# Mixers' queries, keys and probabilities turned in 32x32 squares through HBM, low weight parts last in each unit, and blank matmuls at the opening

## The chip, the cores and the metric

One core of one Trainium2 chip. The metric is the device time of one execution in microseconds, the median of three runs. The core has TensorE (PE), VectorE (DVE), ScalarE (ACT), GpSimd (POOL) and SyncE (SP), which run side by side and wait for one another by semaphores; transfers run on 16 DMA engines and are issued from a queue of SP or POOL here.

## The reference, cut to what matters

Two layers on 256 tokens of width 2048, float32. Layer 0 mixes by retention (8 heads) and neighbourhood attention (8 heads), layer 1 by differential attention (8 heads with two softmax maps each). Each layer then attends to 256 memory tokens and runs a SwiGLU FFN.

```
for i in range(DEPTH):
    h = rms_norm(x, norm_mix_g[i])
    x = x + (retention_na_mixer if i % 2 == 0 else diff_attention_mixer)(h, ...)
    m = rms_norm(mem, norm_mem_g[i])
    x = x + memory_cross_attention(rms_norm(x, norm_xattn_g[i]), m, ...)
    x = x + swiglu_ffn(rms_norm(x, norm_ffn_g[i]), w_ffn_in[i], w_ffn_out[i])
# differential attention, per head:
a = softmax(q0 k0^T * scale + alibi) - lam * softmax(q1 k1^T * scale + alibi)
o = rms_norm(a @ v, out_g) * (1 - lam_init)
```

Queries and keys are normalised per head of 128 in both attentions.

## The kernel before, in words

**Products.** Every projection is a `gemm` (L297) over units. A unit is 256 rows of a weight by 512 columns, against all 256 tokens. Weight and activation are each held as a high part (rounded to fp32r) and a low part (the rest), and three products are summed: high by high (L321), high by low weight (L322), low by high weight (L323). With two halves of tokens (t) and two k-tiles (j) a unit is twelve matmuls with 512 columns each. There are 864 units. `prepare` (L269) loads raw weights by SP's queue, 512 rows at a time, ScalarE casts the high part `wh` (L292), and VectorE subtracts to get the low part `wl` (L293); `LOOK` = 2 units are prepared ahead.

**Side work.** Norms, attention heads and gates are generators in a list (`Side`, L33). After each unit `pump` runs one step of the first task that is due and ready; a `yield n` puts the next step n units later. At most `CAP` = 5 tasks may be under way. `drain` runs named tasks to their end at once. The order of the instructions on each engine is the order in which this writes them.

**Turning.** A matmul needs its operands with features on the partitions, so queries, keys, probabilities, heads' outputs and gates are turned. Two ways are in the kernel. In the first PE transposes 128x128 blocks against an identity into PSUM: `turn` (L345) for queries, keys (`z`) and gates (`sg`), four to a group; `transpose_p` (L545) for probabilities (`pr`); L702 for the outputs of differential attention (`do`). ScalarE and VectorE then take the high and low parts out of PSUM. In the second, `regroup` (L377), used for blocks of x and the FFN's activations, VectorE transposes 32x32 squares within partitions (L389), SP's queue writes the block to a scratch `zd` in HBM (L391), and `LAND` = 2 units later four reads by POOL's queue (L394) bring the squares back to `zz` with partitions exchanged. `MOVE` = 5 units after the write ScalarE and VectorE split it into high and low parts.

**Mixers.** `retention_na` (L613) goes through four groups of four heads, two of neighbourhood attention and two of retention; `normed_T` (L481) squares, sums, takes the reciprocal root by POOL (L334) and scales, `plain_T` does so without a norm, `heads_T` turns. `attend` (L548) makes scores, softmax, turned probabilities and the product. `diff_attention` (L706) goes through four groups b of two heads, by `diff_head` (L662). Their outputs go to `oT`, which the output projection reads. POOL and SP run their queues in order: a DMA that waits for another's landing holds back what stands behind it.

## Time and profile before

| | us |
|---|---|
| median of 3 runs | 2476.86 (2475.91 to 2476.88) |
| profiled execution, its own time | 2475.84 |
| span of the profiled execution | 2474.1 |
| TensorE busy | 2456.3 |
| VectorE busy | 1475.7 |
| ScalarE busy | 1187.0 |
| GpSimd busy | 138.2 |

How to read it: the span runs from the first to the last instruction of one profiled execution. Busy time counts an engine's instructions with overlaps taken once; matmuls are pipelined, so one that is listed with 389 ns can be followed by the next after 227 ns. DMA issues count on POOL as busy; those of SP are only listed as issues. The rows that the prediction rests on stand in a section below.

### The profile page before, as it was taken

How to read it: one execution, taken by the hardware profiler on the slowest of the kernel's cores; microseconds unless marked ns; L12 is line 12 of the kernel's file. 1: busy time of each engine (PE TensorE's matmuls, PEld its weight loads, DVE VectorE, ACT ScalarE, POOL GpSimd, SP SyncE). 2: the span in 40 equal slices, each digit the busy share in tenths (PEclk: the TensorE clock that was granted, in tenths of full speed). 3: DMA queues.
4: the chain of work that ended last, by engine and by line, in shares of the span. 5: the costliest groups of instructions: out<-in, count | busy, mean ns of one | idle time of the engine just before them, and what ended most of it. 6: DMA issues, size and time to landing. Idle time of an engine off the chain costs nothing.

```text
span 2474.1 us, 28641 instructions
## 1 busy us (share of the span) xinstructions
PE 2456.3 (99%) x11184; PEld 2037.1 (82%) x11184; DVE 1475.7 (60%) x1833; ACT 1187.0 (48%) x1538; POOL 138.2 (6%) x215
## 2 busy tenths in 40 slices
PE   8999999999999999999999999999999999999999
PEld 6888888888888888888888888888888888888887
DVE  6775565675655555555567766767655545555554
ACT  6554464564443444444455555655544444443443
POOL 1000001010000000000010000010100000000000
PEclk9999999999999999999999999999999999999999
DMA  8555567656765666566674555675766656665665
GB/s 288 177 169 179 175 226 245 214 192 213 233 216 200 205 212 225 194 198 226 225 241 164 170 170 168 212 249 171 237 222 210 215 188 214 228 206 200 207 217 175
DMA packets 250184, 511.82 MB, mean 207 GB/s; under 512 B 11328, under 2 KB 11968, under 8 KB 250048
## 3 DMA queue, kind: packets, MB, share of 16 engines
q1 hardware_dynamic: 239568, 484.47, 58.5%
q0 software_dynamic: 8320, 23.08, 4.1%
q10 hardware_dynamic: 2160, 2.44, 0.3%
q8 instruction: 87, 1.43, 0.2%
q14 instruction: 49, 0.40, 0.0%
HBM read 486.88 MB, written 23.07 MB: 206 GB/s over the span
## 4 chain that ended last, share of the span: by engine, by line
PE 92%; DMA 3%; DVE 3%; ACT 1%; POOL 1%; issue 0%; ACTq 0%; SPq 0%; POOLq 0%; DVEq 0%
PE acc L322 30%; PE acc L321 30%; PE acc L323 30%; DMA zz<-zd 2%; DVE wl L293 1%; DMA zd<-zz 1%; PE pt L345 1%; ACT wh L292 0%; PE pt L545 0%; PE pa_s L437 0%; PE pa_s L436 0%; DVE x_sb L741 0%; PE pa_s L435 0%; POOL zz L394 0%; PE pa_r L595 0%
## 5 line engine op out<-in xcount | busy, mean ns | idle before, releaser
L293 DVE TENSOR_TENSOR wl<-raw,wh 128x1024 fp32r<-128x1024 f32 (+1 forms) x865 | 1053.7, 1221 | 870.8 <-ACT wh L292 870.4
L292 ACT CAST wh<-raw 128x1024 fp32r<-128x1024 f32 (+1 forms) x865 | 909.1, 1051 | 1158.2 <-PE acc L323 1132.8
L322 PE MATMUL acc<-wl,hTfh 128*128 128x512 f32 x1408 | 547.9, 389 | 0.6 <-DVE wl L293 0.6
L323 PE MATMUL acc<-wh,hTfl 128*128 128x512 f32 x1408 | 547.7, 389 | 0.0
L321 PE MATMUL acc<-wh,hTfh 128*128 128x512 f32 x1408 | 547.7, 389 | 0.0
L321 PE MATMUL acc<-wh,hTh 128*128 128x512 f32 x832 | 332.0, 399 | 9.8 <-ACT wh L292 8.3
L322 PE MATMUL acc<-wl,hTh 128*128 128x512 f32 x832 | 325.7, 391 | 0.9 <-DVE wl L293 0.9
L323 PE MATMUL acc<-wh,hTl 128*128 128x512 f32 x832 | 325.8, 392 | 0.0
L322 PEld LDWEIGHTS acc<-wl,hTfh 128*128 128x128 f32 x1408 | 264.3, 188 | 56.2 <-DVE wl L293 1.4
L323 PEld LDWEIGHTS acc<-wh,hTfl 128*128 128x128 f32 x1408 | 264.3, 188 | 54.9
L321 PEld LDWEIGHTS acc<-wh,hTfh 128*128 128x128 f32 x1408 | 264.3, 188 | 54.9
L322 PE MATMUL acc<-wl,aTh 128*128 128x512 f32 x704 | 274.0, 389 | 0.2 <-DVE wl L293 0.2
L323 PE MATMUL acc<-wh,aTl 128*128 128x512 f32 x704 | 273.9, 389 | 0.0
L321 PE MATMUL acc<-wh,aTh 128*128 128x512 f32 x704 | 273.9, 389 | 0.0
L321 PEld LDWEIGHTS acc<-wh,hTh 128*128 128x128 f32 x832 | 157.2, 189 | 40.0 <-ACT wh L292 8.3
L323 PEld LDWEIGHTS acc<-wh,hTl 128*128 128x128 f32 x832 | 156.7, 188 | 34.0
L322 PEld LDWEIGHTS acc<-wl,hTh 128*128 128x128 f32 x832 | 157.2, 189 | 31.2 <-DVE wl L293 1.8
L394 POOL DMA_DIRECT2D zz<-zd x160 | 87.3, 552 | 1589.9 <-DMA zd<-zz 1410.9
L322 PEld LDWEIGHTS acc<-wl,aTh 128*128 128x128 f32 x704 | 132.1, 188 | 28.2 <-DVE wl L293 0.8
L321 PEld LDWEIGHTS acc<-wh,aTh 128*128 128x128 f32 x704 | 132.1, 188 | 27.5
L323 PEld LDWEIGHTS acc<-wh,aTl 128*128 128x128 f32 x704 | 132.1, 188 | 27.3
L321 PE MATMUL acc<-wh,oTh 128*128 128x512 f32 x256 | 100.2, 392 | 0.0
(189 smaller groups left out, 1940.3 us busy)
## 6 DMA issues: line engine op xcount, KB each, us to landing
raw<-in_w_ffn_in SPq DMA_DIRECT2D x176, 1024.0 KB, 5.1
raw<-in_w_ffn_out SPq DMA_DIRECT2D x88, 1024.0 KB, 5.1
raw<-in_w_in_ab SPq DMA_DIRECT2D x55, 1024.0 KB, 5.2
raw<-in_w_in_c SPq DMA_DIRECT2D x48, 1024.0 KB, 5.2
zd<-zz SPq DMA_DIRECT2D x40, 512.0 KB, 3.8
zz<-zd POOLq DMA_DIRECT2D x160, 128.0 KB, 5.4
raw<-in_w_out_ab SPq DMA_DIRECT2D x16, 1024.0 KB, 5.1
raw<-in_w_xkv SPq DMA_DIRECT2D x16, 1024.0 KB, 5.0
```

The source lines that it names most:

```text
L292: nc.scalar.copy(wh[:, js], raw[:, rs])
L293: nc.vector.tensor_sub(wl[:, js], raw[:, rs], wh[:, js])
L321: nc.tensor.matmul(acc[t], lhsT=hi[:, kt, ts], rhs=wh[:, j], start=first and j == 0, stop=False)
L322: nc.tensor.matmul(acc[t], lhsT=hi[:, kt, ts], rhs=wl[:, j], start=False, stop=False)
L323: nc.tensor.matmul(acc[t], lhsT=lo[:, kt, ts], rhs=wh[:, j], start=False, stop=last and j == 1)
L345: nc.tensor.transpose(pt[:, j, t * P:(t + 1) * P], srcs[t][:, c:c + P], ident)
L394: nc.gpsimd.dma_start(zT[32 * j:32 * j + 32].rearrange("a (i n) -> a i n", i=4), zd[:, :, j].rearrange("i a n -> a i n"))
```

## The change

1. `regroup` takes a number of blocks (`nk` = 4 for 128x1024, 2 for 128x512), a room and a wait. Thirty-five new blocks go through it with `SLOW` = 8 units between write and split: queries and keys of layer 0's four groups and of groups 0 to 2 of differential attention, one of the two gates, the probabilities of 8 neighbourhood heads, and the probabilities and outputs of 6 differential heads. Fifteen are 128x1024 (512 KB), twenty 128x512 (256 KB). The rooms are blocks of `oT` not yet written, `m8` or `qT`.
2. All writes to `zd` (40 before, 75 now) are issued from POOL's queue and not from SP's.
3. In a unit, the eight matmuls with `wh` come first, the four with `wl` last.
4. The operands of a gemm (`pair`) are four tiles of four k-tiles and not one of sixteen.
5. Sixteen 128x128 matmuls of a zeroed tile stand at the opening, ahead of the first unit.
6. `CAP` is 7. In `diff_head` two scalings (32 instructions) go from VectorE to ScalarE; the gains of moved blocks are applied by ScalarE in place.

The diff, cut to its core:

```diff
-LAND, MOVE = 2, 5
+LAND, MOVE, SLOW = 2, 5, 8
-    CAP = 5
+    CAP = 7
...
+    blank = const.tile([P, P], F32, name="blank")
+    nc.vector.memset(blank, 0.0)
+    for _ in range(4):
+        idle = ps_t.tile([P, 2, T], F32, tag="pt", name="idle")
+        for j in range(2):
+            for t in range(2):
+                nc.tensor.matmul(idle[:, j, t * P:(t + 1) * P], lhsT=blank, rhs=blank, start=True, stop=True)
...
-            for t in range(2):
-                ts = slice(t * P, (t + 1) * P)
-                for j in range(2):
-                    kt = kts[u // 2] + 2 * (u % 2) + j
-                    nc.tensor.matmul(acc[t], lhsT=hi[:, kt, ts], rhs=wh[:, j], start=first and j == 0, stop=False)
-                    nc.tensor.matmul(acc[t], lhsT=hi[:, kt, ts], rhs=wl[:, j], start=False, stop=False)
-                    nc.tensor.matmul(acc[t], lhsT=lo[:, kt, ts], rhs=wh[:, j], start=False, stop=last and j == 1)
+            for low in (False, True):
+                for t in range(2):
+                    ts = slice(t * P, (t + 1) * P)
+                    for j in range(2):
+                        hi, lo = src.at(kts[u // 2] + 2 * (u % 2) + j)
+                        if low:
+                            nc.tensor.matmul(acc[t], lhsT=hi[:, ts], rhs=wl[:, j], start=False, stop=last and j == 1)
+                            continue
+                        nc.tensor.matmul(acc[t], lhsT=hi[:, ts], rhs=wh[:, j], start=first and j == 0, stop=False)
+                        nc.tensor.matmul(acc[t], lhsT=lo[:, ts], rhs=wh[:, j], start=False, stop=False)
...
+    def regroup(srcs, room="v", nk=4, wait=MOVE):
+        zt, zT = room_for(room, nk * T)
+        zv = zt.rearrange("p (j k t b) -> p j k t b", j=4, k=nk, t=2)
+        for t in range(2):
+            nc.vector.transpose(zv[:, :, :, t], srcs[t].rearrange("p (k j a) -> p j k a", j=4, a=32))
+        zd = dram.tile([4, 32, 4, nk * 64], F32, tag=f"zd{nk}", name="zd")
+        nc.gpsimd.dma_start(zd.rearrange("i a j n -> (i a) (j n)"), zt)
         yield LAND
         for j in range(4):
             nc.gpsimd.dma_start(zT[32 * j:32 * j + 32].rearrange("a (i n) -> a i n", i=4),
                                 zd[:, :, j].rearrange("i a n -> a i n"))
-        yield MOVE - LAND
+        yield wait - LAND
...
+    def heads_T(zs, dst, g, room=None):
+        if room:
+            zT = yield from regroup(zs, room, wait=SLOW)
+            if g is not None:
+                flat = zT.rearrange("p i k t b -> p (i k t b)")
+                nc.scalar.activation(flat, flat, AF.Copy, scale=g)
+            split_moved(dst, zT)
+            return
...
-        yield 3
-        aT = transpose_p(p0)
+        if room:
+            zT = yield from regroup([p0[:, t] for t in range(2)], "m8", 2, SLOW)
+            aT = tuple(pp.tile([P, 2, T], F32R, name="p" + x) for x in "hl")
+            split_moved(aT, zT)
+        else:
+            yield 3
+            aT = transpose_p(p0)
...
-            nc.vector.tensor_scalar(do[:, t], po[:, t], rr[:, t:t + 1], None, op0=ALU.mult)
+            nc.scalar.activation(do[:, t], po[:, t], AF.Copy, scale=rr[:, t:t + 1])
+        if room:
+            zT = yield from regroup([do[:, t] for t in range(2)], room, 2, SLOW)
...
+            split_moved(oT.at(2 * h, 2), zT)
+            return
```

Where it moves instructions. TensorE, before, in layer 0's first projection: part of one unit, the turning of a block `z` of four heads, and the start of the next unit (`acc_553` and `acc_554` are the two token halves of one accumulator).

```order
L321 MATMUL acc_554<-wh,hTh 128x512
L322 MATMUL acc_554<-wl,hTh 128x512
L323 MATMUL acc_554<-wh,hTl 128x512
L345 MATMUL pt<-ident,z 128x128 x4
L321 MATMUL acc_553<-wh,hTh 128x512
L322 MATMUL acc_553<-wl,hTh 128x512
L323 MATMUL acc_553<-wh,hTl 128x512
```

The same engine after the change, at the same part of the program: one whole unit and the first two rows of the next.

```order
L348 MATMUL acc_585<-wh,hTh 128x512
L349 MATMUL acc_585<-wh,hTl 128x512
L348 MATMUL acc_585<-wh,hTh 128x512
L349 MATMUL acc_585<-wh,hTl 128x512
L348 MATMUL acc_586<-wh,hTh 128x512
L349 MATMUL acc_586<-wh,hTl 128x512
L348 MATMUL acc_586<-wh,hTh 128x512
L349 MATMUL acc_586<-wh,hTl 128x512
L346 MATMUL acc_585<-wl,hTh 128x512 x2
L346 MATMUL acc_586<-wl,hTh 128x512 x2
L348 MATMUL acc_585<-wh,hTh 128x512
```

The low weight part is used from the ninth matmul on and not from the second, and no transposes of `z` stand between units; in the whole program 104 transposes by PE are left of 304.

GpSimd (POOL), before, in differential attention: the end of the reads of x's blocks, and then only the reciprocal roots of the norms of queries and keys (`rr`) and of outputs (`rrd`).

```order
L394 DMA zz<-zd 32x4x256 x4
L334 TENSOR_TENSOR rr<-rr,mhalf 128x8 x2
L334 TENSOR_TENSOR rrd<-rrd,mhalf 128x2 x2
L334 TENSOR_TENSOR rr<-rr,mhalf 128x8 x2
L334 TENSOR_TENSOR rrd<-rrd,mhalf 128x2 x2
```

The same queue after the change, within the same phase (L422 writes a block, L425 reads a part of it back, L360 is the root).

```order
L422 DMA zd<-zz 128x512
L425 DMA zz<-zd 32x4x128 x4
L360 TENSOR_TENSOR rr<-rr,mhalf 128x8
L422 DMA zd<-zz 128x1024
L425 DMA zz<-zd 32x4x256
L422 DMA zd<-zz 128x512
L425 DMA zz<-zd 32x4x256 x2
L425 DMA zz<-zd 32x4x128 x4
L425 DMA zz<-zd 32x4x256
L360 TENSOR_TENSOR rrd<-rrd,mhalf 128x2
L422 DMA zd<-zz 128x512
L425 DMA zz<-zd 32x4x128 x2
```

The roots now stand behind writes and behind reads that wait for a write's landing, and issues of several blocks are interleaved.

## Rows read from the trace of the kernel before

**Rows 1.** Page, part 1: busy time, share of the span, instructions

```profile
PE 2456.3 (99%) x11184; PEld 2037.1 (82%) x11184; DVE 1475.7 (60%) x1833; ACT 1187.0 (48%) x1538; POOL 138.2 (6%) x215
```

**Rows 2.** Windows: busy us of each engine, granted clock, DMA share, GB/s

```profile
124.00:186.00 62.00, 62.00 (x305) 51.86 (x305) 48.37 (x73) 35.29 (x57) 1.63 (x1) 1.00 0.51 168
496.00:558.00 62.00, 61.98 (x309) 51.73 (x309) 48.74 (x78) 38.52 (x72) 7.36 (x13) 1.00 0.61 197
```

**Rows 3.** Waits of TensorE: who for whom, us, times, longest

```profile
PE acc L322 <- DVE wl L293: 2.2, 6, 0.5
...
PE acc L321 <- DVE z L475: 1.5, 2, 0.8
```

**Rows 4.** Groups by form, TensorE: busy us, mean ns, idle before

```profile
L345 PE MATMUL pt<-ident,z 128*128 128x128 f32 x160 | 23.6, 272 | 0.0
```

**Rows 5.** Timeline of TensorE, 115 to 124 us: start, duration, instruction

```profile
115.41 0.39 PE L321 MATMUL acc<-wh,hTh 128*128 128x512 f32 x1
...
118.13 0.39 PE L321 MATMUL acc<-wh,hTh 128*128 128x512 f32 x1
...
119.49 0.60 PE L345 MATMUL pt<-ident,z 128*128 128x128 f32 x4
119.85 0.48 PE L321 MATMUL acc<-wh,hTh 128*128 128x512 f32 x1
...
122.70 0.60 PE L345 MATMUL pt<-ident,z 128*128 128x128 f32 x4
```

**Rows 6.** Timeline of TensorE at the opening, and at the ninth unit

```profile
8.28 0.80 PE L321 MATMUL acc<-wh,hTh 128*128 128x512 f32 x1 [8.28 <-ACT wh L292]
9.49 0.80 PE L322 MATMUL acc<-wl,hTh 128*128 128x512 f32 x1 [0.42 <-DVE wl L293]
10.08 0.63 PE L323 MATMUL acc<-wh,hTl 128*128 128x512 f32 x1
10.51 0.63 PE L321 MATMUL acc<-wh,hTh 128*128 128x512 f32 x1
...
14.32 0.39 PE L321 MATMUL acc<-wh,hTh 128*128 128x512 f32 x1
...
33.36 0.40 PE L321 MATMUL acc<-wh,hTh 128*128 128x512 f32 x1
```

**Rows 7.** Timeline of ScalarE at the ninth unit's weights

```profile
31.01 1.05 ACT L292 CAST wh<-raw 128x1024 fp32r<-128x1024 f32 x1 [3.35 <-DMA raw<-in_w_in_ab]
```

**Rows 8.** Groups by form, VectorE

```profile
L293 DVE TENSOR_TENSOR wl<-raw,wh 128x1024 fp32r<-128x1024 f32 x863 | 1052.4, 1222 | 870.8 <-ACT wh L292 870.4
...
L389 DVE STREAM_TRANSPOSE zz<-sg 128x512 f32<-128x512 f32 x44 | 28.5, 685 | 0.0
...
L697 DVE TENSOR_SCALAR do<-pa_d,rrd 128x256 f32<-128x256 f32 x16 | 7.0, 480 | 6.7 <-POOL rrd L334 6.7
...
L677 DVE TENSOR_SCALAR pr<-pr,rc 128x256 f32<-128x256 f32 x16 | 4.9, 350 | 0.2
```

**Rows 9.** Line L394 (reads): issue ns, landing; last row landing of writes, L391

```profile
L394 POOL DMA_DIRECT2D zz<-zd x160: 550/550/595, 402.9 to 2413.1; - x160
...
DMA to landing us min/median/max: 2.8/5.4/9.4
...
DMA to landing us min/median/max: 2.6/3.8/7.3
```

**Rows 10.** Timelines of 618 to 640 us: VectorE, GpSimd and ScalarE, one FFN block

```profile
621.36 1.29 DVE L389 STREAM_TRANSPOSE zz<-sg 128x512 f32<-128x512 f32 x2
...
626.97 2.17 POOL L394 DMA_DIRECT2D zz<-zd  x4 [71.25 <-DMA zd<-zz]
...
635.09 1.13 ACT L429 CAST aTh<-zz 128x512 fp32r<-128x512 f32 x2
```

**Rows 11.** Waits of all engines: who for whom, us, times, longest

```profile
DVE rr L487 <- POOL rr L334: 27.8, 16, 1.8
...
ACT hTfh L419 <- DMA zz<-zd: 9.4, 5, 3.6
```

More of the change, by code (lines that the diff above doesn't have):

```diff
@@ L558, in attend @@
             nc.vector.tensor_scalar(pr[:, t], pr[:, t], rc[:, t:t + 1], None, op0=ALU.mult)
-        yield g.get("wait", 4)
-        pT = transpose_p(pr)
+        if room:
+            zT = yield from regroup([pr[:, t] for t in range(2)], room, 2, SLOW)
+            pT = tuple(pp.tile([P, 2, T], F32R, name="p" + x) for x in "hl")
+            split_moved(pT, zT)
+        else:
+            yield g.get("wait", 4)
+            pT = transpose_p(pr)
         yield 1, lambda: "v" in g
@@ L605, in ret_head, with gate_T @@
                 head_scale(ro[t], ro[t], rr, t)
-    def gate_T(zs, oT, kt, g):
-        for u in range(2):
-            pt = turn(zs, u)
-            gained_pair(part(oT, slice(kt + 2 * u, kt + 2 * u + 2)), pt, g)
-            yield 0
+    def gate_T(zs, oT, kt, g, room):
+        yield from heads_T(zs, oT.at(kt, 4), g, room)
     def retention_na(j, hT, rstd, oT, gate):
+        spare = [oT.which + x for x in "01"]
         groups = [{"n": 0} for gi in range(4)]
-        groups[0]["tb"] = side.add(na_bias(j, 0, groups[0], hT[0][:, 4, 0:16].bitcast(F32)), 6)
+        groups[0]["tb"] = side.add(na_bias(j, 0, groups[0], hT.blk(1)[0][:, 0, 0:16].bitcast(F32)), 6)
         tails = []
@@ L707, in diff_attention, with spare @@
         groups = [{} for _ in range(4)]
+        def spare(b, x):
+            return oT.which + x if b < 3 else None
         def epi(i, acc):
@@ L712, in epi @@
             if part == 0:
-                g["q"], g["tq"] = normed_T(acc, rstd, c_dq + j, "qT")
+                g["q"], g["tq"] = normed_T(acc, rstd, c_dq + j, "qT", spare(b, "3"))
             elif part == 1:
-                g["k"], g["tk"] = normed_T(acc, rstd, c_dk + j, "kT")
-                g["tasks"] = [side.add(diff_head(g, hh, 2 * b + hh, j, oT), cond=prepared(g)) for hh in range(2)]
+                g["k"], g["tk"] = normed_T(acc, rstd, c_dk + j, "kT", spare(b, "2" if b < 2 else "3"))
+                g["tasks"] = [side.add(diff_head(g, hh, 2 * b + hh, j, oT, oT.which + str(b + 1) if b < 3 else None), cond=prepared(g)) for hh in range(2)]
             else:
@@ L796, in trunk_kernel @@
         ssr = new_ss("ssx")
[L797 removed]
+        tasks = [t for b in range(4) for t in feed_x(hT, b, 1, layer, ssr, ("v", "v", "qT", "m8")[b])]
         g = {"wait": 3}
@@ L831, in act_T @@
             zT = yield from regroup(zs)
-            for t in range(2):
-                split(*(x[:, kt:kt + 4, t * P:(t + 1) * P].rearrange("p k (i b) -> p k i b", i=4) for x in aT),
-                      zT[:, :, :, t].rearrange("p i k b -> p k i b"))
+            split_moved(aT.at(kt, 4), zT)
         for g0, g1 in FFN_GROUPS:
```

86 lines of the change are left out of this document (49 added, 37 removed).

## The prediction

> **What bounds the kernel now.** I read the page's busy shares first [rows 1]: TensorE is busy 2456.3 of 2474.1 us, VectorE 60%, ScalarE 48%, GpSimd 6%. Shares are averages, so I then read two of the fullest stretches [rows 2]: PE is busy 61.98 and 62.00 of 62 us there, VectorE 48.4 and 48.7. PE is the bound in every stretch, and VectorE, at 79%, is the next in the attention phases. So time is won only by taking work, or waits, from PE. Its waits are small [rows 3]: six for low weight parts (2.2 us together), two for an accumulator (1.5 us), besides the wait for the first weights, which ends at 8.28 us [rows 6].
>
> **Part 1, transposes leave PE.** The new order has 104 128x128 transposes where the old had 304: 112 of queries and keys, 56 of probabilities, 24 of outputs, 8 of a gate go. Each is listed at 272 ns [rows 4], but durations on PE overlap, so I go by starts [rows 5]. A unit with no transposes takes 115.41 to 118.13 = 2.72 us for its twelve matmuls. A unit that begins with a group of four takes 119.49 to 122.70 = 3.21 us. A group costs 0.49 us, of which 0.36 passes until the next matmul starts (119.85) and the rest lies in the matmuls behind it. 200 transposes are 50 groups: 50 x 0.49 = **-24.5 us**. Bounds: 50 x 0.36 = 18 us if the rest were not theirs, and 200 x 0.272 = 54 us if each were worth its whole duration. I take 24.5, since the two starts of one unit measure it directly.
>
> The Trainium skill ("TensorE: Matmul & The Clock Gate", Part 4: PE-mode transpose) puts a 128x128 transpose at about 275 ns in a kernel's context. The rows agree on the duration (272 ns) and not on what it costs: by the page's figure the sum would lose 55 us and not 24.5.
>
> **Part 2, low parts last.** The same twelve matmuls per unit; the four with low weight parts come last, so the first of them is ninth and not second. Between two matmuls of one unit the start-to-start time is the same whichever weight or accumulator follows, so the order itself costs nothing. The low part may arrive seven matmuls later, 7 x 0.227 = 1.6 us, while the longest such wait is 0.5 us [rows 3]. All six go: 2.2 us, of which 0.4 is the first unit's and is counted in part 3: **-1.8 us** (bounds 0 and -2.2). The two accumulator waits stay, as they hang on the evacuation of a finished block.
>
> **Part 3, the opening.** The first unit takes 8.28 to 14.32 = 6.04 us [rows 6] where a later one takes 2.72. Its matmuls start 0.43 us apart (10.08, 10.51), nearly twice the later 0.227: I read that as the lower of the two levels (1.2 and not 2.4 GHz), after PE had done nothing for 8 us. Sixteen blank matmuls now start at about 1 us. Four 128x128 transposes take 0.60 us in all [rows 5], so, counting a blank matmul like a transpose, sixteen take at most 2.4 us, at half clock 4.8 us: they end before the weights at 8.28 and delay nothing. If each cost its whole 272 ns [rows 4] at half clock, they would end at 9.7 and cost 1.4 us. Whether PE still runs at the upper level at 8.28, after 2 to 5 us of rest, no row shows. If it does, 3.3 us are to be had in this unit, but the gain meets the next late weight: the ninth unit's high part is cast at 31.01 to 32.06 [rows 7] and PE begins it at 33.36 [rows 6], so beyond 1.3 us the gain turns into waiting for weights. If the clock stays low, the first unit no longer waits for the low part, whose first matmul starts 1.21 us after the one ahead (9.49): 1.21 - 0.43 = 0.8 us are saved. I take **-1.1 us**, bounds -3.3 and +1.4.
>
> **Part 4, what the 35 new squares cost.** Fifteen are 128x1024 and twenty 128x512. Each adds two 32x32 transposes on VectorE (0.69 us for 512 columns [rows 8]), a write and four reads on POOL's queue, and a split on ScalarE and VectorE that replaces one of equal size out of PSUM. VectorE also loses 32 scalings (16 of 0.35 and 16 of 0.48 us [rows 8]) to ScalarE. I count about 15 x 1.38 + 20 x 0.7 - 13.3 + 2 = 23 us more on VectorE, and on ScalarE 32 scalings at 0.48, 13 gains at the 1.05 us of a 1024-column cast [rows 7] and 12 at half of it, 35 us more: estimates from those rows, spread over the attention phases. It costs nothing while VectorE has its 13 us in 62 to spare [rows 2]; if that cover were gone it would be paid in full.
>
> POOL issues 75 writes and 300 reads where it issued 160 reads. At 0.55 us each [rows 9] that adds some 118 us to an engine busy for 138, so no shortage of time, but POOL's queue runs in order. Reads wait for their write to land, and behind them stand other squares' issues and the reciprocal roots of the norms, for which VectorE waits in order (27.8 us in 16 waits now, at most 1.8 us each [rows 11]), with the low weight parts behind it.
>
> How long is the chain? By the landing rows [rows 9]: write 3.8, four issues 2.2, reads 5.4, together 11.4 us; at worst 7.3 + 2.2 + 9.4 = 18.9 us. The squares of today's FFN show it as a timeline [rows 10]: VectorE transposes at 621.36, the reads are issued at 626.97, and ScalarE begins its split at 635.09, 13.7 us and five units behind, without a wait. ScalarE waits for squares only 9.4 us in five cases, at most 3.6 us [rows 11]. In the new order the split stands six to seven units (16 to 19 us) behind the transposes for the large squares, and four, in a few cases three, for the small ones (8 to 11 us): short of the typical chain, though the smaller block should land sooner. A late split delays PE only if it outlasts what PE has ahead: two prepared units, 5.4 us. By this count four consumers are tight: two key squares (about 1.5 us of PE each) and one or two probability squares with three units (about 2 us together). I take **+5 us**, bounds 0 and +20 (35 squares at 0.57 us).
>
> **Sum.** 2475.84 (the profiled execution's own time: span 2474.1 and 1.7 us around it) - 24.5 - 1.8 - 1.1 + 5 = 2453.4. The median lies 1.0 us above that execution, so 2454. What is late next: PE still, with its matmuls.
>
> **Rivals.**
> (a) *Slower: POOL's queue makes the squares late.* PE would wait at the consumer of each square. The gains come to 27.4 us, so 27.4 / 35 = 0.8 us a square eats them, and from (27.4 + 5) / 35 = 0.93 us a square it is slower by over 0.2%. Worst landings plus four foreign issues give 18.9 + 2.2 = 21.1 us against the 16 to 19 us of the large squares and less for the small: late by 2 us or more. At 2 us for half of the 35 that is 36 us on top of the forecast, 2490. For it: small squares with three or four units, and diff attention, where reads and roots share the queue. Against: today's squares [rows 10, 11], and the two units ahead.
> (b) *VectorE becomes the bound in the attention phases.* If half of its extra 23 us comes out as PE time: 2454 + 12 = 2466. For it: 79% busy now, in-order waits for POOL's roots. Against: its low parts may now come 1.6 us later.
> (c) *POOL cannot issue while VectorE streams.* If each of a new square's five issues waited for one subtraction of 1.22 us [rows 8], the chain grows by 6.1 us to 17.5 us typically; if ten of the small squares are late by 3 us that gives 2454 + 30 = 2484. Against: 160 issues took 550, at most 595 ns [rows 9], with VectorE 60% busy.
> The Trainium skill ("SBUF — State Buffer", Summary: rules for kernel authors) has such a rule: a transfer issued by GpSimd starves for descriptors while VectorE is in its faster modes, and should be issued from ScalarE's or SyncE's queue. It speaks against moving the writes; the 595 ns at most do not bear it out, though they time the issue alone.
> (d) *The blank work does nothing, or the low parts' waits remain:* 1 to 3 us worse, 2456; inside the range.
> (e) *Transposes are worth their whole duration:* 2454 - 30 = 2424.
>
> **How the numbers follow.** Forecast with (d): 0.66. (b) 0.15, (a) 0.11, (c) 0.05, (e) 0.03. 0.2% is 5 us, about what a measurement can tell from no change. Faster, below 2471.9: forecast and (e), nearly all of (b) and a fifth of (a), 0.86. Within 0.2%: 0.06, of (a), (b) and (c). Slower, above 2481.8: 0.08. The likeliest case's own range is 2447 (waits 0, opening -3.3) to 2469 (waits +20 and the rest at its value). Widened a little at the low end for the transposes' upper bound, 2444 to 2469 leaves out (e), most of (a) and (c), and the tail of (b).
>
> **What would show it.** PE's rows: 104 transposes, about 30 us less listed busy time, starts of 0.227 us in units that held groups. PE's waits: none left for low parts; new ones, if any, for split products of squares (scores and products), about 5 us together. The first unit's starts at 0.227 if the blank work holds the clock, 0.43 if not. POOL's issues still at 550 ns, or longer if (c) holds. VectorE's share in the attention stretches below 90%, or close to full with low-part waits if (b) holds. The forecast is wrong if waits of PE for squares sum to more than 20 us.

## The result and the profile after

The changed kernel takes **2484.2 us** (median of 5 runs, 2482.3 to 2491.6), the kernel before 2476.2 beside it: ratio 1.0042, 95% interval 1.0028 to 1.0055. It is slower by 0.4%, where 2454 (2444 to 2469) was forecast, so the prediction was wrong by 30 us and in its sign. The profiled execution took 2482.3 us, its span 2480.5.

The page of the changed kernel: span, busy time by engine, shares of the chain that ended last.

```profile
span 2480.5 us, 29244 instructions
PE 2444.7 (99%) x11016; PEld 2023.9 (82%) x11016; DVE 1492.5 (60%) x1886; ACT 1209.3 (49%) x1609; POOL 263.1 (11%) x430
PE 85%; DMA 5%; issue 3%; DVE 3%; ACT 2%; POOL 2%; ACTq 0%; DVEq 0%; POOLq 0%
```

Beside [rows 1]: TensorE has 11.6 us less busy time, but is idle for 2480.5 - 2444.7 = 35.8 us, where it was 2474.1 - 2456.3 = 17.8. The work did leave PE, and waiting took its place. (The trace has 320 transposes before and 120 after; 16 of blocks of x come on top of the 304 and 104 that the change was described with, and 200 leave as said.) Where, the starts of the first matmul of a unit tell (worked out from all matmul records; "best" is the fastest kernel of the experiments, e17):

| units | before, us | after, us | best, us | work in it |
|---|---|---|---|---|
| 0 to 96 | 300.8 | 290.7 | 286.6 | from the first unit's first matmul: layer 0's mixer |
| 96 to 120 | 70.9 | 75.2 | 74.7 | its last heads, output projection |
| 456 to 552 | 300.3 | 310.3 | 297.1 | differential attention |
| the rest of the span | 1802.1 | 1804.3 | 1805.3 | memory attention, FFNs, both ends |

In layer 0 the change first wins 10 us. In differential attention, where 96 transposes (24 groups) leave and 24 x 0.49 = 11.8 us should be won, it loses 10. Stretches of 62 us in that phase, before and then after (busy time and instructions of PE, PEld, DVE, ACT and POOL, granted clock, share of the DMA engines, GB/s):

```profile
1302.00:1364.00 62.00, 61.20 (x308) 51.15 (x307) 45.85 (x75) 36.01 (x61) 4.68 (x4) 1.00 0.49 162
1426.00:1488.00 62.00, 62.00 (x302) 51.92 (x301) 42.45 (x62) 32.23 (x50) 3.97 (x3) 1.00 0.51 171
1550.00:1612.00 62.00, 62.00 (x302) 52.04 (x301) 49.33 (x80) 39.47 (x77) 2.06 (x4) 1.00 0.59 207
```

```profile
1302.00:1364.00 62.00, 58.65 (x260) 48.24 (x261) 45.20 (x71) 34.32 (x54) 13.37 (x19) 0.97 0.69 214
1426.00:1488.00 62.00, 58.73 (x265) 48.32 (x264) 42.06 (x68) 37.36 (x63) 21.86 (x34) 0.97 0.74 221
1550.00:1612.00 62.00, 58.27 (x278) 48.07 (x278) 41.19 (x65) 41.41 (x85) 5.92 (x10) 0.97 0.58 194
```

PE now has holes of 3 to 4 us in each of these, and its clock shows 0.97 of full speed; in the two stretches between them the holes are 2.3 and 2.6 us and the clock 1.00. VectorE is no busier than before, so it is not short of time. What the holes end with, by the waits of the changed kernel (engine, line and what it waited for: us in total, times, longest):

```profile
PE acc L348 <- ACT wh L315: 10.2, 9, 1.9
PE acc L348 <- DVE z L519: 5.1, 2, 2.6
PE acc L346 <- DVE wl L316: 2.7, 3, 1.3
PE pa_d L472 <- ACT ph L466: 1.9, 1, 1.9
ACT ph L466 <- DMA zz<-zd: 33.9, 10, 7.4
ACT zz L754 <- DMA zz<-zd: 21.6, 6, 6.4
ACT zz L501 <- DMA zz<-zd: 18.4, 8, 3.5
ACT do L749 <- POOL rrd L360: 14.0, 7, 4.4
```

PE's own waits for split products (`ph`, `pl`, `kTh`, `kTl`) come to 6.4 us, before 1.6. It waits most for weights (`wh`, 10.2 us, of which 3.6 lie in the opening), and the engine that casts them, ScalarE, waits for squares. Over all its rows ScalarE waits 104.3 us for reads of squares, before 15.6. One such place, ScalarE's timeline in differential attention (start, us, engine, line, instruction, then in brackets the idle time before it and what ended it):

```profile
1535.43 0.71 ACT L466 CAST ph<-zz 128x256 fp32r<-128x256 f32 x2 [5.00 <-DMA zz<-zd]
...
1536.54 1.04 ACT L315 CAST wh<-raw 128x1024 fp32r<-128x1024 f32 x1
...
1542.83 0.84 ACT L749 ACTIVATE do<-pa_d,rrd 128x256 f32<-128x256 f32 x2 [4.38 <-POOL rrd L360]
1543.56 2.94 ACT L315 CAST wh<-raw 128x1024 fp32r<-128x1024 f32 x3
...
1551.78 0.84 ACT L749 ACTIVATE do<-pa_d,rrd 128x256 f32<-128x256 f32 x2 [4.40 <-POOL rrd L360]
1552.51 1.05 ACT L315 CAST wh<-raw 128x1024 fp32r<-128x1024 f32 x1
```

The split of a square of probabilities waits 5.00 us for its reads, and then the scaling of an output twice waits 4.4 us for a root of POOL. Each time a weight's cast stands right behind. At 1543.56 three casts in a row show how far ScalarE had fallen behind. PE pays for it in pieces: 1.11 us of waiting for a low part at 1542.30, 0.33 and 0.83 us for weights at 1557.15 and 1565.19, and 1.93 us for `ph` at 1580.30. The second wait for the root comes from a square as well, by POOL's timeline of the same stretch:

```profile
1548.84 2.18 POOL L425 DMA_DIRECT2D zz<-zd  x4 [3.79 <-DMA zd<-zz]
1551.03 0.72 POOL L360 TENSOR_TENSOR rrd<-rrd,mhalf 128x2 f32<-128x2 f32 x1
```

POOL waits 3.79 us for a write to land before it issues the reads, and the root stands behind them. VectorE's timeline shows how little time the split of that same square (`do`, turned at 1543.34) is given:

```profile
1543.34 0.81 DVE L420 STREAM_TRANSPOSE zz<-do 128x256 f32<-128x256 f32 x2 [1.10 <-ACT do L749]
1544.64 3.50 DVE L316 TENSOR_TENSOR wl<-raw,wh 128x1024 fp32r<-128x1024 f32 x3 [0.49 <-ACT wh L315]
...
1553.59 1.23 DVE L316 TENSOR_TENSOR wl<-raw,wh 128x1024 fp32r<-128x1024 f32 x1 [0.49 <-ACT wh L315]
...
1555.88 0.76 DVE L467 TENSOR_TENSOR oTl<-zz,oTh 128x256 fp32r<-128x256 f32 x2
```

Between the transposes and the split stand four weight subtractions, so four units, though the code writes `SLOW` = 8. Counted so over the built program, queries and keys have 4 to 8 units, layer 0's probabilities 4 to 6, those of differential attention 3 to 5, its outputs 3 to 5; the FFN's squares of the kernel before have 6, where the code writes 5. The order on an engine is thus not only the order in which the code is written: the build moves a split ahead of its place.

### The profile page after: what moved, and what is told of

Same layout as the page of the kernel before. It is cut to its first block, busy times and chain, and to the rows that moved or that the text cites. A ratio compares the mean times of both kernels' runs of the same rounds, so it can differ in the third digit from the quotient of the medians.

```text
span 2480.5 us, 29244 instructions
## 1 busy us (share of the span) xinstructions
PE 2444.7 (99%) x11016; PEld 2023.9 (82%) x11016; DVE 1492.5 (60%) x1886; ACT 1209.3 (49%) x1609; POOL 263.1 (11%) x430
## 4 chain that ended last, share of the span: by engine, by line
PE 85%; DMA 5%; issue 3%; DVE 3%; ACT 2%; POOL 2%; ACTq 0%; DVEq 0%; POOLq 0%
PE acc L348 28%; PE acc L349 28%; PE acc L346 27%; DMA zz<-zd 2%; DVE wl L316 1%; ACT wh L315 1%; DMA zd<-zz 1%; POOL zz L425 1%; POOL rr L360 1%; DMA raw<-in_w_in_ab 1%; DMA raw<-in_w_xq 0%; PE pa_s L473 0%; ACT pr L581 0%; PE pa_s L474 0%; PE pa_s L472 0%
## 5 line engine op out<-in xcount | busy, mean ns | idle before, releaser
L346 PE MATMUL acc<-wl,hTfh 128*128 128x512 f32 x1408 | 376.3, 389 | 0.0
L348 PE MATMUL acc<-wh,hTh 128*128 128x512 f32 x832 | 327.4, 393 | 14.2 <-ACT wh L315 9.1
L346 PE MATMUL acc<-wl,hTh 128*128 128x512 f32 x832 | 224.7, 392 | 2.7 <-DVE wl L316 2.7
L422 POOL DMA_DIRECT2D zd<-zz x75 | 42.7, 570 | 1646.2 <-DVE zz L420 1591.5
L425 POOL DMA_DIRECT2D zz<-zd x300 | 164.5, 555 | 229.0 <-DMA zd<-zz 104.5
L346 PE MATMUL acc<-wl,aTh 128*128 128x512 f32 x704 | 188.1, 389 | 0.0
```

Of the source, the lines that this page charges most:

```text
L346: nc.tensor.matmul(acc[t], lhsT=hi[:, ts], rhs=wl[:, j], start=False, stop=last and j == 1)
L348: nc.tensor.matmul(acc[t], lhsT=hi[:, ts], rhs=wh[:, j], start=first and j == 0, stop=False)
L422: nc.gpsimd.dma_start(zd.rearrange("i a j n -> (i a) (j n)"), zt)
L425: nc.gpsimd.dma_start(zT[32 * j:32 * j + 32].rearrange("a (i n) -> a i n", i=4), zd[:, :, j].rearrange("i a n -> a i n"))
```

## The experiments

All ratios are to the kernel before on the same chip; its medians lay between 2475.0 and 2476.2 us. Each kernel has 4 to 11 runs.

**One part alone.** e1 is the kernel before with the blank matmuls only.

```diff
+    blank = const.tile([P, P], F32, name="blank")
...
+                nc.tensor.matmul(idle[:, j, t * P:(t + 1) * P], lhsT=blank, rhs=blank, start=True, stop=True)
```

> The kernel before with the sixteen blank matmuls alone. In the trace of the change the first unit takes 2.94 us and not 6.04, so the blank work does raise the clock; but PE then waits 1.66 us at the ninth unit for weights and 2.53 us at 54.7 us for an accumulator, and is 1.5 us later than before at the seventeenth unit. Theory (the gain meets late weights): between -1.5 and +0.5 us against the kernel before, with the first unit at 2.9 us and a new wait of 1 to 2 us at the ninth. Rival (the opening as predicted, -1.1 to -3.3 us): faster by 2 us or more, no new wait.

Measured 2477.3, ratio 1.0008 (0.9999 to 1.0017): nothing won, and +1.9 us (-0.2 to +4.2), which is not clear of the noise. The opening of the changed kernel shows where the gain goes: on PE the first unit's first matmul, the second unit's and the ninth unit's, and on ScalarE the cast of the ninth unit's weights:

```profile
1.06 5.64 PE L121 MATMUL idle<-blank 128*128 128x128 f32 x32 [1.06 <-DVE blank L116]
8.61 0.50 PE L348 MATMUL acc<-wh,hTh 128*128 128x512 f32 x1 [1.90 <-ACT wh L315]
...
11.55 0.39 PE L348 MATMUL acc<-wh,hTh 128*128 128x512 f32 x1
...
33.03 0.50 PE L348 MATMUL acc<-wh,hTh 128*128 128x512 f32 x1 [1.66 <-ACT wh L315]
...
31.93 2.00 ACT L315 CAST wh<-raw 128x1024 fp32r<-128x1024 f32 x2 [5.65 <-DMA raw<-in_w_in_ab]
```

The clock was held: the first unit takes 8.61 to 11.55 = 2.94 us, before 6.04 [rows 6]. The 3.1 us are gone by the ninth unit, which begins at 33.03 (before 33.36 [rows 6]), since its raw weights come no earlier: their cast starts at 31.93, before at 31.01 [rows 7]. In e1's own trace, with the unit's old order, the first unit takes 8.21 to 12.08 = 3.87 us, 0.76 of it a wait for a low part, and the ninth begins at 33.20. Next to nothing of the gain is left by then; why e1 would be slower, if it is, stays open.

e2 is the kernel before with the low parts last in each unit, e6 the same with the low parts last within each half of the tokens.

```diff
-            for t in range(2):
-                ts = slice(t * P, (t + 1) * P)
-                for j in range(2):
...
+            for low in (False, True):
+                for t in range(2):
+                    ts = slice(t * P, (t + 1) * P)
+                    for j in range(2):
...
+                        if low:
+                            nc.tensor.matmul(acc[t], lhsT=hi[:, kt, ts], rhs=wl[:, j], start=False, stop=last and j == 1)
+                            continue
```

e6 differs from e2 in the loops' order alone:

```diff
-            for low in (False, True):
-                for t in range(2):
-                    ts = slice(t * P, (t + 1) * P)
+            for t in range(2):
+                ts = slice(t * P, (t + 1) * P)
+                for low in (False, True):
```

> The kernel before with the low weight parts last in each unit, nothing else. The prediction's step: 1.8 us faster, the waits for low parts gone. Rival read from the trace of the change: the first token half of a block is now complete after ten matmuls and not after six, so the block's sums start later and the wait for its accumulator (0.72 us before at 56.03, 2.53 us after at 57.62) grows, at 1301 us likewise: +3.6 us for the two, net about +1 to +2 us.

> The kernel before with the low parts last within each token half: per half two high by high, two low by high, then two by the low part, so that the first half of a block is complete after six matmuls again. Theory (low parts last cost 12 us because a block's first half is complete four matmuls later, ScalarE's squares of the block fall behind a cast that waits for the eighth matmul of a unit, and PE waits for the accumulator): at most 3 us from the kernel before, waits for the accumulator back near 1.5 us in two. Rival (the cost lies in the release of the weight buffers, or in TensorE's order itself): still 6 us or more slower.

e2 took 2487.5, ratio 1.0047 (1.0035 to 1.006): the order that "costs nothing" costs 12 us. In e2 the first token half of a finished block is complete after ten matmuls of its last unit and not after six. The squares of the norm (`sq`) then come behind a cast that itself waits for PE. ScalarE at the end of the first query block of differential attention, before and in e2:

```profile
1300.54 0.60 ACT L470 ACTIVATE sq<-acc 128x512 f32<-128x512 f32 x1 [0.30 <-PE acc L323]
1301.90 1.05 ACT L292 CAST wh<-raw 128x1024 fp32r<-128x1024 f32 x1 [0.76 <-PE acc L323]
1302.86 0.59 ACT L470 ACTIVATE sq<-acc 128x512 f32<-128x512 f32 x1
```

```profile
1306.07 1.05 ACT L292 CAST wh<-raw 128x1024 fp32r<-128x1024 f32 x1 [1.67 <-PE acc L326]
1307.02 0.59 ACT L473 ACTIVATE sq<-acc 128x512 f32<-128x512 f32 x1
1308.79 1.05 ACT L292 CAST wh<-raw 128x1024 fp32r<-128x1024 f32 x1 [1.18 <-PE acc L326]
1309.74 0.59 ACT L473 ACTIVATE sq<-acc 128x512 f32<-128x512 f32 x1
```

The root, the scaling and with them the accumulator's release come later, and PE, which waited 0.80 us there before, now waits 2.62:

```profile
1314.99 0.47 PE L325 MATMUL acc<-wh,hTh 128*128 128x512 f32 x1 [2.62 <-DVE z L478]
...
1316.32 0.63 PE L325 MATMUL acc<-wh,hTh 128*128 128x512 f32 x1
1316.74 0.63 PE L326 MATMUL acc<-wh,hTl 128*128 128x512 f32 x1
```

The matmuls behind that wait start 0.42 us apart and not 0.227, and the granted clock over these 5 us is 0.66 of full speed (columns as in the stretches above):

```profile
1314.00:1319.00 5.00, 4.01 (x11) 3.18 (x12) 3.73 (x6) 1.33 (x2) 0.00 (x0) 0.66 0.32 124
```

So a stall can cost more than its length. The two waits of PE for a finished block's accumulator account for 3.6 of the 12 us (5.1 against 1.5); nine short waits of transposes for `z` add 1.8, slower matmuls some more, and the rest wasn't taken apart. e6 keeps PE's order by halves: 2476.5, ratio 1.0005 (0.9997 to 1.0014), and its waits for that accumulator fall from 5.1 to 0.6 us. So the loss came with the late first half: e6 gives the low parts less time than e2 and the high parts' buffers back later, and still doesn't lose. But nothing is won either: the 1.8 us of waits for low parts don't show in the time.

e7 has the squares alone: the changed kernel with the order of the unit as before and no blank work. The 32 scalings stay on ScalarE.

```diff
-            for low in (False, True):
...
+                    nc.tensor.matmul(acc[t], lhsT=hi[:, ts], rhs=wh[:, j], start=first and j == 0, stop=False)
+                    nc.tensor.matmul(acc[t], lhsT=hi[:, ts], rhs=wl[:, j], start=False, stop=False)
+                    nc.tensor.matmul(acc[t], lhsT=lo[:, ts], rhs=wh[:, j], start=False, stop=last and j == 1)
```

> The change with the old order of matmuls in a unit and without the blank work: squares, their writes on POOL's queue, finer tiles, scalings on ScalarE. Theory (the parts add up): 2484 - 12 (low parts last alone) - 1.5 (blank alone) = about 2470.5 us. Rival (with squares the low parts' order costs less, since waits overlap): 2476 or more. The prediction's sum for this part was -24.5 + 5: 2456.

Measured 2495.4, ratio 1.0078 (1.0064 to 1.0092): slower than the whole change, though the order taken out of it costs 12 us by itself. The parts don't add. With late squares the weights' low parts are late too, and the old order, which wants one as the second matmul, pays for it; the new order hides it. TensorE's waits in e7 (8.5 of the first row are the first weights at the opening; the profiled run is the slowest of six, 2499.7):

```profile
PE acc L335 <- ACT wh L306: 19.7, 8, 8.5
PE acc L336 <- DVE wl L307: 17.6, 23, 2.7
```

**Where the squares go, and who writes them.** e3 is the changed kernel with the writes on SP's queue as before. e4 has no new squares in differential attention, e9 only its queries and keys (with the unit's old order, no blank, scalings on VectorE), e5 the same as e9 but only layer 0's squares.

```diff
-        nc.gpsimd.dma_start(zd.rearrange("i a j n -> (i a) (j n)"), zt)
+        nc.sync.dma_start(zd.rearrange("i a j n -> (i a) (j n)"), zt)
...
-            return oT.which + x if b < 3 else None
+            return None
...
-                g["tasks"] = [side.add(diff_head(g, hh, 2 * b + hh, j, oT, oT.which + str(b + 1) if b < 3 else None), cond=prepared(g)) for hh in range(2)]
+                g["tasks"] = [side.add(diff_head(g, hh, 2 * b + hh, j, oT, None), cond=prepared(g)) for hh in range(2)]
...
-            nc.scalar.activation(do[:, t], po[:, t], AF.Copy, scale=rr[:, t:t + 1])
+            nc.vector.tensor_scalar(do[:, t], po[:, t], rr[:, t:t + 1], None, op0=ALU.mult)
```

The first pair is e3; the second (queries and keys of differential attention) is in e4 and e5; the third (its probabilities and outputs) in e4, e5 and e9; the last (one of the two scalings) in e5 and e9.

> The change with the writes of squares back on SP's queue. Theory A (ScalarE and VectorE wait in order for squares that come too late by their place in the program; who issues the write matters little): within 3 us of the change, about 2482 us. Theory B (POOL's queue is the trouble: writes and roots stand behind reads that wait for a landing): 8 us or more faster than the change, with ScalarE's wait for the root of the outputs (14.0 us in 7) down to under 5 us. Against both, SP's queue holds the weights' loads behind a write that waits for VectorE: if that bites, slower than the change by some us, with new waits for raw weights.

Measured 2491.7, ratio 1.0063 (1.005 to 1.0077): by the medians 7.5 us slower than with POOL's queue, though the two intervals just overlap. So the writes' place on POOL's queue is not what makes the change slow; its reads and roots stayed there in every run, so their part isn't isolated. The trace of the changed kernel shows POOL's issues undisturbed (count; duration in ns, min/median/max; first and last start):

```profile
L422 POOL DMA_DIRECT2D zd<-zz x75: 548/561/615, 60.2 to 2413.3; - x75
```

```profile
L425 POOL DMA_DIRECT2D zz<-zd x300: 548/550/802, 64.6 to 2418.4; - x150
```

Landings are no slower either: the medians are 3.3 us for writes and 5.0 for reads, before 3.8 and 5.4 [rows 9]. Rival (c) is out. Why e3 is slower stays open: ScalarE's waits for raw weights are not longer in it (14.2 us, 22.1 in the change).

> The change with differential attention's queries, keys, probabilities and outputs turned by PE again (24 groups of four transposes, 24 x 0.49 = 11.8 us of PE back). In the unit clock the change loses 10 us against before between units 456 and 552, where it should have won 11.8, so the squares there cost about 22 us. Theory (the loss is there): 2484 - 22 + 12 = about 2474 us, 10 us faster than the change, PE's waits in 1300 to 1590 us down to a few. Rival (the loss is spread over all that the change does, or is the clock's): within 3 us of the change or slower by up to 12.

> As the kernel with layer 0's squares only, plus the six blocks of queries and keys of differential attention; probabilities and outputs there stay on PE. Theory (the large squares pay, with six to seven units of slack; it is the small ones with three or four and the drains at the phase's end that cost): 12 groups x 0.49 = 5.9 us less than that kernel, about 2460. Rival (any square in differential attention costs more than it saves, as roots and reads share POOL's queue): at or above it.

> The kernel before plus the squares of layer 0 only (26 groups of transposes fewer), with finer tiles and writes on POOL's queue; old order of matmuls, no blank work, scalings on VectorE, differential attention turned by PE. Theory (layer 0's squares are worth nearly their transposes): 26 x 0.49 = 12.7 us less and some 2 us of new waits: about 2465. Rival (every new square costs PE about what it saves): within 3 us of the kernel before.

e4 took 2476.7 (1.0007, 0.9998 to 1.0016), 7.6 us less than the change with 24 more groups of transposes on PE: by this estimate the squares of differential attention cost about 11.8 + 7.6 = 19 us, more than they take away. PE's waits account for 11.7 of them (31.0 in the change, 19.3 in e4). e9 took 2482.1 (1.0033, 1.0022 to 1.0044), e5 2481.2 (1.0022, 1.0013 to 1.003): even layer 0's alone lose in the old order. With low parts last by half, and e5's other edits, layer 0's alone (e12) reach 2477.1 (1.0009, 1.0 to 1.0018), level with before:

> The same with eight units of slack. Layer 0's squares gave -11 us on top of low parts last (2487.5 to 2476.6) and +6 us on top of the old order (2475.4 to 2481.2). Theory (with the old order the low part has no slack when VectorE waits in order; half-wise gives some): between 2466 and 2476, slower than the same kernel with twelve units. Rival (only the full deferral of the low parts helps): about 2481.

**More slack.** My first theory was that eight units are too few. e10 is the changed kernel with twelve, e13 all squares and e11 layer 0's squares with twelve, both with low parts last by half, no blank and scalings on VectorE.

```diff
-LAND, MOVE, SLOW = 2, 5, 8
+LAND, MOVE, SLOW = 2, 5, 12
```

> The change with twelve units between a square's write and its split (8 in the change). The chain from write to landing is as long in the change (8 to 18.6 us, medians about 12) as before the change, but ScalarE waits 104 us for squares, up to 7.4 us at once, with casts of weights behind each wait. Theory (too little slack in the program's order; ScalarE in order holds the weights): ScalarE's waits for squares fall below 50 us and the time to 2479 or less. Rival (the drains at a phase's end, and not the eight units, set the distance): waits and time within 3 us of the change, or slower in differential attention, where more of the work is left to the drain.

> All squares of the change, twelve units of slack, low parts last within each token half, no blank work, scalings on VectorE. Theory (differential attention's squares cost more than they save, since its heads follow one another closely and the phase ends in a drain): 5 us or more slower than the kernel with layer 0's squares only. Rival (with enough slack and the half-wise order all squares pay): 5 us or more faster than that kernel, near 2457.

> Layer 0's squares only, twelve units of slack, low parts last within each token half, no blank work, scalings on VectorE. Theory (the half-wise order keeps a block's first half early and gives low parts 0.7 us, and twelve units hide the squares): the 26 groups' 12.7 us come out less 3: about 2466. Rival (each layer-0 square costs what it saves, as in the kernel with layer 0's squares alone): 2476 to 2481.

e10: 2495.2 (1.0079, 1.0065 to 1.0093); e13: 2495.5 (1.0082, 1.0068 to 1.0095); e11: 2484.9 (1.004, 1.0028 to 1.0053), 7.8 us worse than e12. The theory fell: more slack on paper is slower. The built order says why in part: with twelve units asked, the probabilities and outputs of differential attention still stand only 3 to 6 subtractions ahead of their split, and ScalarE's waits for squares stay (107.5 us in e10). In layer 0 some splits do come later, up to 9 units for probabilities and 12 for one block of queries, and PE now waits at the squares' consumers. In e10 the largest row of PE's waits is one that the change does not have, the output projections' wait for split outputs:

```profile
PE acc L348 <- ACT oTh L466: 6.6, 2, 4.2
```

Beside it stand 7.3 us for `ph` and `pl` (4.3 in the change); the waits of PE grow by 8.2 us in all, of the 11 us lost. In e11 PE waits 10.1 us for `ph` and `pl`, 3.9 in e12. The rest stays open; a room used again before its write has landed is one thing seen, in e11 VectorE waits 5.42 us for that ahead of a transpose.

**Splits held in their place.** In e14 the split of each new square (with its gain) is made to queue on ScalarE and VectorE behind the weight's cast and subtraction last issued where it stands in the code; nothing else changes. e17 is e14 with low parts last by half of the tokens. e15 is e17 without blank work and with the scalings on VectorE, e16 is e15 with layer 0's squares only, e18 is e15 with the unit's old order.

```diff
-            nc.scalar.copy(wh[:, js], raw[:, rs])
-            nc.vector.tensor_sub(wl[:, js], raw[:, rs], wh[:, js])
+            at["cast"] = nc.scalar.copy(wh[:, js], raw[:, rs])
+            at["sub"] = nc.vector.tensor_sub(wl[:, js], raw[:, rs], wh[:, js])
...
+    def held():
+        stack = ExitStack()
+        stack.enter_context(tc.issue_after(at["cast"].ins))
+        stack.enter_context(tc.issue_after(at["sub"].ins))
+        return stack
...
-            split_moved(aT, zT)
+            with held():
+                split_moved(aT, zT)
```

> The change with every split of a new square (and its gain) queued on ScalarE and VectorE behind the cast and the subtraction that the code had issued when it reached the split. In the change's built order the split stands ahead of its place in the code: 4 to 6 subtractions of weights between transposes and split for layer 0's probabilities, 3 to 5 for differential attention's small squares, where the code asks for eight units; held, these are 6 to 7 and 4 to 7, and twelve units asked for in an earlier run had left them at 3 to 6 for most. Theory (ScalarE waits in order for squares that it meets too early): ScalarE's waits for squares fall from 104 to below 60 us and the time by 6 us or more against the change, to 2478 or less. Rival (the chain itself is too long for its consumers, and a later split makes scores and products late instead): the waits move from ScalarE to PE's products, time within 3 us of the change or slower.

> The same with low parts last within each token half, no blank work, scalings on VectorE: the parts that cost by themselves taken out. Theory: 2475 - 24.5 + some 8 us of waits left = about 2460, faster than the kernel before. Rival (squares in the mixers cost what they save in whatever order): 2475 or more.

> The same with layer 0's squares only (26 groups). Without the hold this kernel took 2477, with 55 us of waits of ScalarE for squares and two stalls of PE of 4.0 and 3.3 us. Theory: those two stalls go, 2467 or less. Rival: 2475 or more; if it lies below the kernel with all squares held, differential attention's squares cost more than they save even so.

> The changed kernel with the new squares' splits held behind the weights' cast and subtraction, and the low parts last within each half of tokens; the blank work, the 32 scalings on ScalarE and all else stay. The two runs before it differ from one another by three edits (order within the unit, blank work, scalings), 2473 against 2467. Theory: the 6.7 us are the order's, since a block's first half of tokens is again complete after six matmuls: 2466 to 2468, no wait of TensorE for a root of a finished block (2.6 us in one such wait before). Rival: blank work and scalings were the cost: 2472 to 2474, as with the low parts last over the whole unit.

> All 35 squares, splits held, no blank work, scalings on VectorE, and the twelve matmuls of a unit in the order of the kernel before: high by high, high by low, low by high. Against the squares alone without the hold (2495) this tells what the hold gives, against the held kernel with low parts last by half (2467) what that order gives when splits do not come early. Theory: the squares' splits ahead of the weights' casts are the whole loss, and low parts were late only because of them: 2466 to 2470. Rival: low parts are late whenever VectorE has the squares' work too, and the order covers that: 2475 to 2485, with over 8 us of waits of TensorE for low parts (17.6 us without the hold).

| us, median | unit's order as before | low last in the unit | low last by half |
|---|---|---|---|
| squares of before only | 2475 to 2476 | 2487.5 (e2) | 2476.5 (e6) |
| all new squares | 2495.4 (e7) | 2484.2 (the change) | |
| all new squares, held | 2473.9 (e18) | 2473.3 (e14) | 2466.7 (e15), 2463.4 (e17) |
| layer 0's, not held / held | 2481.2 (e5) / | | 2477.1 (e12) / 2468.2 (e16) |

The change, e14 and e17 have the blank work, and their scalings on ScalarE; e7 has its scalings on ScalarE and no blank work; the other kernels with squares in the table have neither. Ratios: e14 0.9991 (0.9982 to 0.9999), e15 0.9965 (0.9951 to 0.9978), e16 0.997 (0.9958 to 0.9981), **e17 0.9956 (0.9943 to 0.9968)**, e18 1.0 (0.9991 to 1.0009).

The hold alone gives 10.9 us to the change (e14) and 8.9 to layer 0's squares by half (e16 against e12). All squares in the old order are 21.5 us faster with it (e18 against e7), but there the scalings go back to VectorE too, and no run parts the two. So the early splits are a cause, and with the order in the unit (9.9 us, below) one of the two that an edit has isolated in the change; the noise does not rank them. In e14 ScalarE waits 40.8 us for squares and not 104.3, and PE's waits fall from 31.0 to 22.7 us, though one of them, for `ph`, is now 5.4 us long. In e17 the `do` block that answers to the one above is turned at 1525.53 and split at 1544.70, with seven weight subtractions between; VectorE's first and last rows of it:

```profile
1525.53 0.76 DVE L420 STREAM_TRANSPOSE zz<-do 128x256 f32<-128x256 f32 x2
1526.21 2.31 DVE L316 TENSOR_TENSOR wl<-raw,wh 128x1024 fp32r<-128x1024 f32 x2
...
1544.70 0.75 DVE L473 TENSOR_TENSOR oTl<-zz,oTh 128x256 fp32r<-128x256 f32 x2
```

TensorE's largest waits in e17, to be read against those of the changed kernel:

```profile
PE acc L348 <- ACT wh L315: 4.1, 4, 2.2
PE acc L346 <- DVE wl L316: 3.0, 5, 1.4
PE pa_d L478 <- ACT ph L472: 2.6, 1, 2.6
...
PE acc L348 <- DVE z L526: 0.3, 1, 0.3
```

The wait for weights falls from 10.2 to 4.1 us, of which 2.7 lie in the opening, and that for `z` from 5.1 to 0.3. e14 and e17 differ by the order alone: 9.9 us, more than the 6.7 that e17 was to explain. e18's time lies between its two expectations. PE's wait for low parts in it is the rival's sign:

```profile
PE acc L336 <- DVE wl L307: 9.8, 13, 1.9
```

With the squares held and the scalings on VectorE these waits fall from 17.6 us (e7) but do not go, so early splits are not the whole reason why low parts are late. In e15, which has them last by half and is else the same, they are 1.6 us. e15 and e17 have the same span in their profiled runs (2463.7); that the blank work or the scalings give the 3.2 us between their medians isn't shown. e16 is within 2 us of e15: held, the squares of differential attention bring next to nothing, though 24 groups of transposes less are on PE; not held, they cost 7.6 us (e4).

## Why the prediction was wrong, point by point

**Part 1 (-24.5): about right.** The number of matmuls of each line times their median start-to-start time sums to 2447.0 us before and to 2425.5 in e7 and e18: 21.5 us less, by starts, as no run takes the transposes away without putting squares in their place. The size measured by starts, and not the whole duration, was the right one; rival (e) is out.

**Part 2 (-1.8, bounds 0 and -2.2): wrong, +12 alone.** The step that failed is "the order itself costs nothing", with "the two accumulator waits stay, as they hang on the evacuation of a finished block". They do hang on it, but the order sets when the block's first half is finished, four matmuls later. I followed who waits for the moved matmuls' inputs, not who waits for their output. e6 shows it by restoring the halves. Where squares are late, the same order is worth having (e7 against the change), so its price in the change can't be given as one number.

**Part 3 (-1.1, bounds -3.3 and +1.4): the mechanism was seen rightly, the size not.** The clock rose and the first unit won 3.1 us; the ninth unit's weights took it back, as the text said they might. Alone it is +1.9 (-0.2 to +4.2), a little above my upper bound of +1.4, with an interval that reaches below it. That the blank work takes 5.64 us and not at most 2.4 or 4.8 delayed nothing.

**Part 4 (+5, bounds 0 and +20): the term that turned the sign.** Squares alone (e7) against before are +20, and with the 21.5 us won by the transposes they cost 41; in the change, parts 2 and 4 together cost 2484.2 - 2476.2 + 21.5 = 29.5 us, up to 2 less for the blank work. The rows and the count of units were nearly right: I named squares with three or four units against a chain of 11.4 us, and the change shows 3 to 5 for the small ones of differential attention and a chain of 3.3 + 2.2 + 5.0 = 10.5 us by its medians. What I priced came out too: PE's waits at the squares' consumers are 6.4 us, 4.8 more than before, where I took 5. The step that failed is the price, "a late split delays PE only if it outlasts what PE has ahead", counted square by square for its consumer, four of them. The consumer isn't the first to pay. A split that waits on ScalarE or VectorE holds the weights' casts behind it, and so every product; so does a scaling moved to ScalarE that waits for its root. Several such waits follow one another (5.00, 4.38 and 4.40 us, ending within 17 us), together more than the 5.4 us prepared. In e7 PE waits 11.2 us for high parts behind the opening (19.7 less 8.5) and 17.6 for low parts, but 3.0 for squares' products. The kernel before has 15.6 us of waits for squares on ScalarE, and PE's waits behind the first weights were 5.3 us in all; the change has 104.3, and 31.0 on PE, 4.6 of them in the opening. The sum on ScalarE is no measure of the time by itself (e11 has 43.0 and is slower than e12 with 55.4), but cutting it at the same splits gave 10.9 us back (e14). My sign of being wrong, waits of PE for squares of more than 20 us in sum, did not show though the forecast failed: it looked at the consumers as well. "None left for low parts" failed too, 2.7 us are.

**The rivals.** (a) had the right kind: late squares. That its price of 2490 is close is luck, as it was worked out from 36 us of waits at the consumers, and these are 6.4 us. The writes on POOL's queue are not the cause (e3); POOL's part that shows is the root behind reads, 14.0 us of ScalarE's waits in seven, and e17, the fastest kernel, still has 15.5 of these. No run moves the reads off POOL's queue, and none moves the scalings alone, so what they cost beside early splits isn't shown. (b) is out: VectorE is 60% busy and has idle time where PE waits. (c) is out by the issue times and the landings. The Trainium skill ("SBUF — State Buffer", Summary: rules for kernel authors) advises issuing from ScalarE's or SyncE's queue rather than GpSimd's while VectorE is in its faster modes; here the issues took 548 to 615 ns for the writes, and the kernel with the writes on SP's queue was slower by the medians (e3). Whether VectorE was in such a mode no row shows.

What is left between e17 and the forecast of 2454 is 9 us. PE's holes, counted as what a start-to-start time has over the median of its line where that is 0.26 us or more, sum to 7.5 us before (the 8.3 us ahead of the first matmul not counted), 35.2 in the change and 22.4 in e17. Of the 22.4, 4.9 stand in the first 62 us, the blank work's pause of 2.4 among them, 7.4 between 1302 and 1550, with one wait of 2.6 us for `ph` as the longest, and the rest is spread; single causes weren't taken apart.

## What to carry to other kernels

When work is moved from the bounding engine into a chain through memory, price the wait of the chain's last step by what is queued behind it on its own engine, and not by its consumer alone; and read in the built order how far apart the steps really stand, since a delay written in the code may not be kept unless an order is forced. When matmuls of one accumulation are reordered, ask when the first output is complete as well as when the inputs are wanted. Parts of a change that are each measured alone may not add: the order that lost 12 us by itself went, together with the blank work, with 11 us less beside late squares.

## What the runs showed of the hardware that was not expected

- After a stall of 2.62 us TensorE's matmuls started 0.42 us apart for some two microseconds (granted clock 0.66 over 5 us, so the lower level, 1.2 GHz, for part of them); after 0.80 us at the same place before, and after 1.90 us behind the blank work, they kept the upper one.
- Sixteen float32 matmuls of 128x128 are listed as 32 and keep PE busy for 5.64 us in the change, 5.28 in e1.
- 375 transfers issued by GpSimd's queue took a median of 550 (reads) and 561 ns (writes) with VectorE 60% busy over the span, the longest 802 ns.
